# Hybrid RG-LRU, S5 and DeltaNet layer: the input scale moved into the S5 weights, the decay columns moved between RG-LRU tiles

## Chip, core and metric

The kernel runs on one core of a Trainium2 chip. The metric is the device time of one execution in microseconds (us), from the runs before: 1097.19 us median.

## What is computed

One layer of a recurrent decoder over 512 prompt and 64 sample positions (8 sequences of 8), 576 columns in all, with 1024 channels:

```python
h = rmsnorm(x, norm_pre_mix)
proj = h @ w_in      # rg_x, rg_gate, s5_u, qkv, z, a_in, b_in, three merge gates
y_rg = (rglru(conv(rg_x)) * gelu(rg_gate)) @ rg_w_out      # gated linear scan
y_s5 = glu(gelu(Re(C s) + D u)) @ s5_w_out                 # complex diagonal scan of u = s5_u
g    = -exp(a_log) * softplus(a_in + dt_bias)              # decay logits, 4 heads
beta = sigmoid(b_in)
y_gd = (rmsnorm(gated_delta(conv(qkv), beta, g)) * silu(z)) @ gdn_w_out
x = x + rmsnorm((g_rg*y_rg + g_s5*y_s5 + g_gd*y_gd) @ w_out, norm_post_mix)
x = x + rmsnorm(swiglu(rmsnorm(x)), norm_post_ffn)
```

The new recurrent states are outputs too. Everything is float32.

## The kernel before

All activations are held transposed: 128 channels on the partitions, 576 positions along the free axis, worked on in two halves of 288. A weight tile of 128 output channels is loaded as 128x512 pieces; ACT rounds a piece to its high part (`wh`, L181), DVE subtracts to get the low part (`wl`, L182), and each product is three matmuls, high by high, high by low and low by high (L199 to L201), into one PSUM tile per half (`mm3`). The input `h` is split in the same way (`hh`, `hl`, L236 and L237).

A tile scheduler lays the instructions out: each engine has one queue that it works through in order, and where several instructions could go next, the one written earlier in the source goes first. PSUM is given out by tags: "mm" (3 buffers, `mmp`) for the large products, "sm" (3 buffers) for the S5 tiles `gtp`, `xp`, `s5yp` and others, "sr" (2 buffers, `sr`).

The **start** loads x (`xa`), the S5 weights (`wr`, `uw`) and two tables (`par`, `con`) on SP's queue. `x_sums` squares x and adds the squares up, and multiplies x in place by the norm's scale `g_pre` (L356, ACT). `x_rows` turns the sums into a row of 1/rms values (`cps`, L365; Newton steps on DVE that end in `rs_o`, L118; spread over the partitions by `rows`, L262). `x_h` multiplies x by that row and splits it (L374). `x_u` computes the S5 input `u`, four tiles of 128 channels for each half, by plain float32 matmuls of the unsplit weights with `xa` (L381), and multiplies the result by the row while it leaves PSUM (L382). `issue_after(marks)` keeps the later `x_u` matmuls behind those of `x_rows`.

Then **S5**: constants of the state-space model on DVE (`s5ar`, L465, and after it exponentials, sines and powers), and for each of four tiles a front (`s5_front`: `bl`, L614 to L616 on DVE; `gtp`, L626, transposes it on PE; `ktp`, L632; `xp`, L648) and a chain (`s5_chain`: scans `zs`, products `zt`, outputs `s5yp`, L699 and L700). The tiles of **RG-LRU** (`rg(0)` to `rg(3)`: a projection, a convolution L420, gate products `gps` L748, a scan L769, a split L236 and L237) follow in the source, then five **merge gates** (`gate`), then the **decay block** (L833 to L905): the eight a and b columns `abps` (L849), their transposes `abc` (L854), exponential and softplus series on 128x20 tiles (L128 and L134 to L160), `gcl` (L871), running sums on PE (`gcps`, L873 to L878), `bgp` (L901), and a store `bgd` (L905) that later loads `eg` and `bet` (L969) read back. Then the merge of the RG-LRU branch (`mg`, L802) and the GDN branch, which begins with the projection and convolution of q and k (`pad`, L407 to L409), `sqp` (L931) and decay products `dt` (L973).

Of the kernel before, what the change touches and what calls it, by code (L numbers as in the profile page):

```python
# [8 lines left out]
F32 = mybir.dt.float32  # L9
# [56 lines left out]
def hybrid_step(ctx: ExitStack, tc: tile.TileContext, i, o, dbg=None):  # L66
# [242 lines left out]

    def acc_tile(name):  # L310
        return ap_.tile([128, KT, NT], F32, name=name, tag="acc")
# [8 lines left out]
    def load_u(m):  # L320
        us_.append(T("u"))
        uw.append([])
        raw = wp.tile([128, KT, 128], F32, name=nm("wr"), tag="wr", bufs=2) if m < 2 else None
        for a in range(0, KT, KC):
            if m < 2:
                r = raw[:, a:a + KC, :]
            else:
                r = sp5.tile([128, KC, 128], F32, name=nm("uw"), tag="PS"[m % 2], bufs=6 - m % 2)
            yield SY.dma_start(r, i["w_in"][IDX["u"] + m][:, a:a + KC, :])
            uw[m] += [r[:, k, :] for k in range(KC)]  # L330

    def load_c(t, src, a, b):
        yield SY.dma_start(t[:, a:b], i[src][:, a:b])

    xl, ul = [load_x(0), load_x(1)], [load_u(m) for m in range(4)]
    p0, p1 = load_c(par, "par", 0, NPAR - NHIST), load_c(par, "par", NPAR - NHIST, NPAR)
    c0, c1 = load_c(con, "con", 0, NCON - NLVL), load_c(con, "con", NCON - NLVL, NCON)
    for g_ in (p0, ul[0], xl[0], xl[0], ul[0], xl[0], xl[0], c0, ul[1], xl[1], xl[1], ul[1], xl[1], xl[1], ul[2], ul[2], ul[3], ul[3],
               p1, c1):
        next(g_, None)  # L340
# [6 lines left out]
    def x_sums(half):  # L347
        sl, sqs = hsl(half), sq_[half]
        for j in range(4):
            xv = xa[:, 2 * j:2 * j + 2, sl]  # L350
            if half and j % 2 == 0:
                S.activation(sqs[j], xv, AF.Square)
            else:
                V.tensor_tensor(sqs[j], xv, xv, op=OP.mult)
            for k in (2 * j, 2 * j + 1):
                S.activation(xa[:, k, sl], xa[:, k, sl], AF.Copy, scale=P("g_pre")[:, k:k + 1])  # L356
        V.tensor_tensor(sqs[0], sqs[0], sqs[1], op=OP.add)
        V.tensor_tensor(sqs[2], sqs[2], sqs[3], op=OP.add)
        V.tensor_tensor(sqs[0], sqs[0], sqs[2], op=OP.add)
# [11 lines left out]
    def x_h(half):  # L371
        for k in range(KT):
            t = R("h")[:, :NH]
            (G if half and k % 4 == 3 else V).tensor_tensor(t, xa[:, k, hsl(half)], rw_[half], op=OP.mult)  # L374
            split(t, h[k][0][:, hsl(half)], h[k][1][:, hsl(half)])

    def x_u(half, m, after=None):
        ps = mmp()
        with tc.issue_after(after) if after else nullcontext():
            for k in range(KT):  # L380
                PE.matmul(ps, uw[m][k], xa[:, k, hsl(half)], start=k == 0, stop=k == KT - 1)  # L381
        V.tensor_tensor(us_[m][:, 0:NT].rearrange("p (j c) -> p j c", j=8)[:, :, 36 * half:36 * half + 36],  # L382
                        ps.rearrange("p (c j) -> p j c", j=8), rw_[half].rearrange("p (c j) -> p j c", j=8), op=OP.mult)

    x_sums(0)
    x_sums(1)
    x_rows(0)
    x_h(0)
    x_u(0, 0)
    x_u(0, 1, marks[0])  # L390
    x_rows(1)
    x_u(0, 2, marks[1])
    x_u(0, 3, marks[2])
    x_h(1)
    for m in range(4):
        x_u(1, m, marks[3])
# [68 lines left out]
    V.tensor_tensor(ar[:, 0:NS], are, dts, op=OP.mult)  # L465
# [246 lines left out]
    V.tensor_scalar(nl_, P("rg_lam"), -1.0, None, op0=OP.mult)  # L712
# [95 lines left out]
    V.tensor_scalar(hb, P("glu_b"), 0.5, None, op0=OP.mult)  # L808
# [24 lines left out]
    rg_h = [rg(m) for m in range(3)]  # L833
    rg_h.append(rg(3))
    g1 = [gate(0, m) for m in range(5)]
# [15 lines left out]
    cps = pss.tile([128, 512], F32, name="abc", tag="sm")  # L851
# [18 lines left out]
    exp_cols(cp, nA, P("a_log"), 4)  # L870
    V.scalar_tensor_tensor(gcl, gcl, -1.0, nA[:, None, :].to_broadcast([128, 5, 4]), op0=OP.mult, op1=OP.mult)  # L871
    cps = pss.tile([128, 512], F32, name="gcps", tag="sm")
# [27 lines left out]
    bgp = pss.tile([128, 512], F32, name="bgp", tag="sm")  # L900
# [5 lines left out]

    DQ.dma_start(o["rg_h"], hout)
# [767 lines left out]
```

## Time and profile before

| | before |
|---|---|
| median of 3 runs | 1097.19 us (1095.03 to 1099.34) |
| profiled execution | 1097.05 us |
| its span | 1095.1 us |
| mean granted TensorE clock | 0.974 of full speed |
| PE busy | 1034.5 us, 94% |
| DVE busy | 795.3 us, 73% |
| ACT busy | 487.3 us, 44% |
| POOL busy | 231.0 us, 21% |

The span is the time between the first and last record of one execution; 1.95 us of the execution's time lie outside it. Matmul records overlap, since each lasts longer than the distance to the next one; the cost of a matmul in a full stream is the distance between starts. PE here is TensorE, DVE is VectorE, ACT is ScalarE, POOL is GpSimd, SP issues most of the loads. A plain float32 matmul leaves two records, the split ones leave one each.

### The profile page before, as it was taken

How to read it: one execution, taken by the hardware profiler on the slowest of the kernel's cores; microseconds unless marked ns; L12 is line 12 of the kernel's file. 1: busy time of each engine (PE TensorE's matmuls, PEld its weight loads, DVE VectorE, ACT ScalarE, POOL GpSimd, SP SyncE). 2: the span in 40 equal slices, each digit the busy share in tenths (PEclk: the TensorE clock that was granted, in tenths of full speed). 3: DMA queues.
4: the chain of work that ended last, by engine and by line, in shares of the span. 5: the costliest groups of instructions: out<-in, count | busy, mean ns of one | idle time of the engine just before them, and what ended most of it. 6: DMA issues, size and time to landing. Idle time of an engine off the chain costs nothing.

```text
span 1095.1 us, 20057 instructions
## 1 busy us (share of the span) xinstructions
PE 1034.5 (94%) x7658; PEld 988.9 (90%) x7658; DVE 795.3 (73%) x1853; ACT 487.3 (44%) x971; POOL 231.0 (21%) x301
## 2 busy tenths in 40 slices
PE   5999999967999999999999899899999999999994
PEld 4799989967989889998899899899999999999994
DVE  7899989876997678743636747875676776867756
ACT  4258943424443433222333444354653635536620
POOL 1024111104532234221001331210111201112114
PEclk8999999988999999999999999999999999999997
DMA  6333223422323133212112621124564646746602
GB/s 204 92 103 103 72 82 83 113 67 92 102 84 90 68 110 101 83 54 107 59 53 69 227 91 58 59 73 130 135 177 95 155 125 135 183 92 140 164 1 87
DMA packets 69521, 112.74 MB, mean 103 GB/s; under 512 B 27434, under 2 KB 35762, under 8 KB 69426
## 3 DMA queue, kind: packets, MB, share of 16 engines
q1 hardware_dynamic: 61650, 97.31, 27.7%
q0 software_dynamic: 7776, 14.16, 8.0%
q8 instruction: 60, 0.98, 0.4%
q14 instruction: 35, 0.29, 0.1%
HBM read 103.20 MB, written 8.24 MB: 102 GB/s over the span
## 4 chain that ended last, share of the span: by engine, by line
PE 78%; DVE 12%; DMA 4%; ACT 3%; issue 2%; POOL 0%; SPq 0%; DVEq 0%; ACTq 0%; POOLq 0%
PE mm L199 11%; PE mm L200 11%; PE mm L201 11%; PE mm L1439 10%; PE mm L1441 10%; PE mm L1440 10%; PE mm L381 2%; DVE wl L182 2%; PE up L1183 1%; PE s5yp L700 1%; DMA wr<-in_w_gate 1%; PE gps L748 1%; PE s5yp L699 1%; ACT wh L181 1%; PE rows L262 1%
## 5 line engine op out<-in xcount | busy, mean ns | idle before, releaser
L181 ACT ACTIVATE wh<-wr 128x512 fp32r<-128x512 f32 x250 | 154.7, 628 | 221.8 <-PE mm L200 119.4
L199 PE MATMUL mm<-hh,wh 128*128 128x288 f32 x768 | 232.8, 304 | 6.8 <-ACT pad L407 5.4
L182 DVE TENSOR_TENSOR wl<-wr,wh 128x512 fp32r<-128x512 f32 x250 | 182.2, 736 | 77.9 <-ACT wh L181 75.5
L200 PE MATMUL mm<-hl,wh 128*128 128x288 f32 x768 | 231.2, 301 | 0.0
L201 PE MATMUL mm<-hh,wl 128*128 128x288 f32 x768 | 230.1, 300 | 0.0
L199 PEld LDWEIGHTS mm<-hh,wh 128*128 128x128 f32 x768 | 145.9, 190 | 12.7 <-ACT pad L407 5.7
L201 PEld LDWEIGHTS mm<-hh,wl 128*128 128x128 f32 x768 | 145.9, 190 | 2.8 <-issue 2.2
L200 PEld LDWEIGHTS mm<-hl,wh 128*128 128x128 f32 x768 | 146.0, 190 | 2.5 <-issue 1.7
L1441 PE MATMUL mm<-fh,wl 128*128 128x288 f32 x352 | 103.7, 295 | 0.0
L1439 PE MATMUL mm<-fh,wh 128*128 128x288 f32 x320 | 94.6, 296 | 0.0
L1440 PE MATMUL mm<-fl,wh 128*128 128x288 f32 x320 | 94.4, 295 | 0.0
L1441 PE MATMUL mm<-hfh,wl 128*128 128x288 f32 x288 | 84.5, 296 | 0.7 <-DMA wl<-in_w_gate 0.7
L1440 PE MATMUL mm<-hfl,wh 128*128 128x288 f32 x288 | 84.9, 295 | 0.0
L1439 PE MATMUL mm<-hfh,wh 128*128 128x288 f32 x288 | 84.8, 295 | 0.0
L199 PE MATMUL mm<-brh,wh 128*128 128x288 f32 x224 | 67.4, 305 | 4.3 <-DVE mg L802 1.8
L200 PE MATMUL mm<-brl,wh 128*128 128x288 f32 x224 | 68.1, 305 | 0.9 <-DVE brl L237 0.6
L201 PE MATMUL mm<-brh,wl 128*128 128x288 f32 x224 | 66.9, 299 | 0.0
L1441 PEld LDWEIGHTS mm<-fh,wl 128*128 128x128 f32 x352 | 66.1, 188 | 0.0
L1440 PE MATMUL mm<-t,wh 128*128 128x288 f32 x216 | 64.0, 297 | 0.0
L1441 PE MATMUL mm<-t,wl 128*128 128x288 f32 x216 | 63.7, 295 | 0.0
L1439 PE MATMUL mm<-t,wh 128*128 128x288 f32 x216 | 63.6, 295 | 0.0
L1439 PEld LDWEIGHTS mm<-fh,wh 128*128 128x128 f32 x320 | 60.0, 188 | 0.1
(501 smaller groups left out, 2575.9 us busy)
## 6 DMA issues: line engine op xcount, KB each, us to landing
wr<-in_w_in SPq DMA_DIRECT2D x48, 512.0 KB, 3.5
wr<-in_w_gate SPq DMA_DIRECT2D x22, 512.0 KB, 3.9
wr<-in_w_up SPq DMA_DIRECT2D x22, 512.0 KB, 4.2
wr<-in_w_down SPq DMA_DIRECT2D x20, 512.0 KB, 4.9
wl<-in_w_gate POOLq DMA_DIRECT2D x27, 256.0 KB, 4.5
wl<-in_w_up POOLq DMA_DIRECT2D x27, 256.0 KB, 4.3
wr<-in_w_out SPq DMA_DIRECT2D x8, 512.0 KB, 3.5
xa<-in_x SPq DMA_DIRECT2D x8, 288.0 KB, 6.3
```

The costliest lines, as they stand in the source:

```text
L181: S.activation(hi, raw, AF.Copy)
L182: (eng or lo_eng()).tensor_tensor(lo, raw, hi.bitcast(F32), op=OP.subtract)
L199: PE.matmul(acc, hi[:, k, :], xh[:, sl], start=k0 + k == 0, stop=False)
L200: PE.matmul(acc, hi[:, k, :], xl[:, sl], start=False, stop=False)
L201: PE.matmul(acc, lo[:, k, :], xh[:, sl], start=False, stop=k0 + k == n - 1)
L262: m0 = PE.matmul(rows[:, 96 * b:96 * b + 96], rc[:96, b:b + 1].to_broadcast([96, 128]), ident[:96, :96], start=True, stop=True).ins
L381: PE.matmul(ps, uw[m][k], xa[:, k, hsl(half)], start=k == 0, stop=k == KT - 1)
L699: PE.matmul(ypv[:, b_, :], tm[:, g, :], x[:, g, :], start=True, stop=False)
L700: PE.matmul(ypv[:, b_, :], cl[g // 4][:, g % 4, 1:9, :].rearrange("p d h -> p (d h)"), st[:, g, :], start=False, stop=True)
L1439: PE.matmul(acc, hi[:, k0 + k, :], xh, start=new and k == 0, stop=False, skip_group_check=not new)
L1440: PE.matmul(acc, hi[:, k0 + k, :], xl, start=False, stop=False, skip_group_check=not new)
L1441: PE.matmul(acc, lo[:, k0 + k, :], xh, start=False, stop=k == len(x) - 1, skip_group_check=not new)
```

## The change

Three things are edited.

**The start.** The scale `g_pre` is no longer applied to x. It is multiplied into the S5 weights in place (`u_gain`, 32 activations of 128x128 in place of 16 of 128x288), and into `h` by a scalar_tensor_tensor that stays on DVE for all 16 pieces (before, two of them went to POOL). The matmuls of `x_u` and its evacuation `x_u_out` are taken apart, and two of the eight products get PSUM tiles of the tag "sr", so that five can be under way before a row of 1/rms values exists. `issue_after` is gone. The `par` table is loaded in three pieces, the first of them (32 columns, with `g_pre`) ahead of all else; S5 weights go ahead of the second half of x; a one-column activation at the very start (`first`) brings in ACT's table. ACT takes six of the eight squares (before two).

**The constants.** `s5ar`, `nlam`, `hb` and `nA` now read `pc`, a tile of zeros that takes the buffer of the second `rs_o`; they stand behind the second half's row in DVE's queue.

**The decay block** stands after `rg(1)` and ahead of `rg(2)`, `rg(3)` and the five gates in the source, and `abc`, `gcps` and `bgp` take PSUM tiles of the tag "sr".

```diff
@@ -307,6 +307,11 @@
+    first = cp.tile([128, 1], F32, name="first")
+    V.memset(first, 0.0)
+    S.activation(first, first, AF.Square)
@@ -326,17 +331,18 @@
-            yield SY.dma_start(r, i["w_in"][IDX["u"] + m][:, a:a + KC, :])
+            d_ = SY.dma_start(r, i["w_in"][IDX["u"] + m][:, a:a + KC, :])
             uw[m] += [r[:, k, :] for k in range(KC)]
+            yield d_
...
-    p0, p1 = load_c(par, "par", 0, NPAR - NHIST), load_c(par, "par", NPAR - NHIST, NPAR)
+    pg, p0, p1 = (load_c(par, "par", a, b) for a, b in ((0, 32), (32, NPAR - NHIST), (NPAR - NHIST, NPAR)))
...
-    for g_ in (p0, ul[0], xl[0], xl[0], ul[0], xl[0], xl[0], c0, ul[1], xl[1], xl[1], ul[1], xl[1], xl[1], ul[2], ul[2], ul[3], ul[3],
-               p1, c1):
+    for g_ in (pg, ul[0], xl[0], xl[0], ul[0], xl[0], xl[0], p0, c0, ul[1], ul[1], xl[1], xl[1], ul[2], ul[2], xl[1], xl[1],
+               ul[3], ul[3], p1, c1):
@@ -348,12 +354,10 @@
-            if half and j % 2 == 0:
+            if half or j % 2:
                 S.activation(sqs[j], xv, AF.Square)
             else:
                 V.tensor_tensor(sqs[j], xv, xv, op=OP.mult)
-            for k in (2 * j, 2 * j + 1):
-                S.activation(xa[:, k, sl], xa[:, k, sl], AF.Copy, scale=P("g_pre")[:, k:k + 1])
@@ -371,29 +375,44 @@
-            (G if half and k % 4 == 3 else V).tensor_tensor(t, xa[:, k, hsl(half)], rw_[half], op=OP.mult)
+            V.scalar_tensor_tensor(t, xa[:, k, hsl(half)], P("g_pre")[:, k:k + 1], rw_[half], op0=OP.mult, op1=OP.mult)
             split(t, h[k][0][:, hsl(half)], h[k][1][:, hsl(half)])
-    def x_u(half, m, after=None):
-        ps = mmp()
-        with tc.issue_after(after) if after else nullcontext():
-            for k in range(KT):
-                PE.matmul(ps, uw[m][k], xa[:, k, hsl(half)], start=k == 0, stop=k == KT - 1)
+
+    def u_gain(m):
+        for k in range(KT):
+            S.activation(uw[m][k], uw[m][k], AF.Copy, scale=P("g_pre")[:, k:k + 1])
+
+    def x_u(half, m):
+        ps = sr("u")[:, 0:NH] if (half, m) in ((0, 3), (1, 0)) else mmp()
+        for k in range(KT):
+            PE.matmul(ps, uw[m][k], xa[:, k, hsl(half)], start=k == 0, stop=k == KT - 1)
+        return half, m, ps
+
+    def x_u_out(half, m, ps):
         V.tensor_tensor(us_[m][:, 0:NT].rearrange("p (j c) -> p j c", j=8)[:, :, 36 * half:36 * half + 36],
                         ps.rearrange("p (c j) -> p j c", j=8), rw_[half].rearrange("p (c j) -> p j c", j=8), op=OP.mult)
+    u_gain(0)
+    pu = [x_u(0, 0)]
     x_sums(0)
+    u_gain(1)
+    pu.append(x_u(0, 1))
     x_sums(1)
+    u_gain(2)
+    pu.append(x_u(0, 2))
     x_rows(0)
+    u_gain(3)
+    pu.append(x_u(0, 3))
+    for p_ in pu:
+        x_u_out(*p_)
     x_h(0)
-    x_u(0, 0)
-    x_u(0, 1, marks[0])
     x_rows(1)
-    x_u(0, 2, marks[1])
-    x_u(0, 3, marks[2])
+    pu = [x_u(1, m) for m in range(3)]
+    for p_ in pu:
+        x_u_out(*p_)
     x_h(1)
-    for m in range(4):
-        x_u(1, m, marks[3])
+    x_u_out(*x_u(1, 3))
...
-    V.tensor_tensor(ar[:, 0:NS], are, dts, op=OP.mult)
+    V.scalar_tensor_tensor(ar[:, 0:NS], are, pc[:, 0:1], dts, op0=OP.add, op1=OP.mult)
...
-    V.tensor_scalar(nl_, P("rg_lam"), -1.0, None, op0=OP.mult)
+    V.tensor_scalar(nl_, P("rg_lam"), -1.0, pc[:, 0:1], op0=OP.mult, op1=OP.add)
...
-    V.tensor_scalar(hb, P("glu_b"), 0.5, None, op0=OP.mult)
+    V.tensor_scalar(hb, P("glu_b"), 0.5, pc[:, 0:1], op0=OP.mult, op1=OP.add)
@@ -830,9 +849,7 @@
-    rg_h = [rg(m) for m in range(3)]
-    rg_h.append(rg(3))
-    g1 = [gate(0, m) for m in range(5)]
+    rg_h = [rg(m) for m in range(2)]
...
-    cps = pss.tile([128, 512], F32, name="abc", tag="sm")
+    cps = sr("abc")
...
-    exp_cols(cp, nA, P("a_log"), 4)
+    V.tensor_scalar(nA, P("a_log"), pc[:, 0:1], None, op0=OP.add)
+    exp_cols(cp, nA, nA, 4)
...
-    cps = pss.tile([128, 512], F32, name="gcps", tag="sm")
+    cps = sr("gcps")
...
-    bgp = pss.tile([128, 512], F32, name="bgp", tag="sm")
+    bgp = sr("bgp")
...
+    rg_h += [rg(m) for m in range(2, 4)]
+    g1 = [gate(0, m) for m in range(5)]
```

The decay block, and with it the S5 fronts, move on PE too. Before, the first S5 front stands among the products of the first merge gate (`mm_2072`, `mm_2073`):

```order
L201 MATMUL mm_2072<-hh_137,wl_2069 128x288
L199 MATMUL mm_2073<-hh_131,wh_2068 128x288
L626 MATMUL gtp_697<-con,bl_686 128x128 x4
L632 MATMUL ktp_703<-cl_691,bb_675 32x128 x4
L748 MATMUL gps_1859<-xc_1846,rgw_1849 128x288
```
and the running sums of the decay stand at the end of the S5 outputs, ahead of the next q or k tile (`mm_3098`):

```order
L699 MATMUL s5yp_1333<-s5x_1108,tm_1117 128x72
L700 MATMUL s5yp_1333<-st_1299,cl_1161 128x72
L873 MATMUL gcps<-gcl,con 128x16
L874 MATMUL gcps<-gcl,con 64x4
L875 MATMUL gcps<-gcl,con 128x16
L876 MATMUL gcps<-gcl,con 64x4
L878 MATMUL gcps<-con,gcl 128x8 x4
L901 MATMUL bgp<-con,bg 40x128
L931 MATMUL sqp_3005<-sq_3003,con 32x288 x2
L199 MATMUL mm_3098<-hh_123,wh_3089 128x288
```
After, the first front stands behind the products of all five gates (`mm_2500` is the last of them), at the first products of the merge (`mm_2575`):

```order
L200 MATMUL mm_2500<-hl_142,wh_2495 128x288
L201 MATMUL mm_2500<-hh_141,wl_2496 128x288
L199 MATMUL mm_2575<-brh_2553,wh_2571 128x288
L199 MATMUL mm_2576<-brh_2553,wh_2571 128x288
L645 MATMUL gtp_717<-con,bl_706 128x128 x4
L199 MATMUL mm_2610<-brh_2553,wh_2606 128x288
```
the running sums stand between the first S5 tile's `xp` products and the gate products of `rg(2)`:

```order
L667 MATMUL xp_773<-s5x_681,gm_716 128x72 x2
L667 MATMUL xp_773<-s5x_681,gm_739 128x72 x2
L891 MATMUL gcps_1851<-gcl,con 128x16
L892 MATMUL gcps_1851<-gcl,con 64x4
L893 MATMUL gcps_1851<-gcl,con 128x16
L894 MATMUL gcps_1851<-gcl,con 64x4
L896 MATMUL gcps_1851<-con,gcl 128x8 x4
L919 MATMUL bgp_1879<-con,bg 40x128
L767 MATMUL gps_2027<-xc_2021,rgw_2024 128x288
```
and the place where they stood reads:

```order
L200 MATMUL mm_3118<-hl_142,wh_3114 128x288
L201 MATMUL mm_3118<-hh_141,wl_3115 128x288
L951 MATMUL sqp_3026<-sq_3024,con 32x288 x2
L199 MATMUL mm_3119<-hh_127,wh_3110 128x288
L200 MATMUL mm_3119<-hl_128,wh_3110 128x288
```
What moved: the decay's PE work stands some 450 instructions earlier, the S5 fronts some 240 later. Between the first front (instruction 690) and the first front of tile 3 (instruction 780) PE has 90 instructions, 36 of them large products; before, 466 instructions lay between those two (448 and 914), most of them large products. From `mm_3119` on (`mm_3098` before) the two programs have the same order.

On DVE the constants that read `pc` stand behind the second row (`rs_o`):

```order
L118 SCALAR_TENSOR_TENSOR rs_o_307<-rs_a_310,rs_y_309 96x3
L182 TENSOR_TENSOR wl_1381<-wr_1378,wh_1380 128x512
L182 TENSOR_TENSOR wl_1385<-wr_1378,wh_1384 128x512
L461 MEMSET s_z 128x3
L463 TENSOR_SCALAR par<-par,s_z 128x48
L182 TENSOR_TENSOR wl_1449<-wr_1446,wh_1448 128x512
L484 SCALAR_TENSOR_TENSOR s5ar_436<-par,s_z,s_dt 128x48
L731 TENSOR_SCALAR nlam<-par,s_z 128x4
L827 TENSOR_SCALAR hb<-par,s_z 128x4
L535 TENSOR_TENSOR s_ci<-par 128x48
L887 TENSOR_SCALAR nA<-par,s_z 128x4
```
Before, `s5ar` and `nlam` stood ahead of the first row:

```order
L712 TENSOR_SCALAR nlam<-par 128x4
L717 TENSOR_SCALAR rgc<-par 128x4
...
L128 SCALAR_TENSOR_TENSOR ex_r_621<-ex_r_621,ex_x_619 128x4
L465 TENSOR_TENSOR s5ar_416<-par,s_dt 128x48
L357 TENSOR_TENSOR sq_143<-sq_143,sq_144 128x576
```
What moved: the constants' whole chain, which stood around the Newton steps of both rows, starts after the second.

## Rows read from the trace of the kernel before

**Rows 1.** The page, busy time of each engine and its instructions.
```profile
PE 1034.5 (94%) x7658; PEld 988.9 (90%) x7658; DVE 795.3 (73%) x1853; ACT 487.3 (44%) x971; POOL 231.0 (21%) x301
```

**Rows 2.** Busy time by stretch: PE, PEld, DVE, ACT, POOL, clock, DMA.
```profile
0.00:52.60 52.60, 40.16 (x163) 31.68 (x164) 43.06 (x191) 19.75 (x41) 4.86 (x14) 0.90 0.46 148
52.60:120.00 67.40, 67.40 (x494) 65.69 (x493) 67.03 (x173) 48.50 (x94) 20.36 (x25) 1.00 0.32 97
189.80:233.50 43.70, 43.70 (x357) 42.58 (x355) 38.03 (x95) 16.63 (x34) 7.69 (x20) 1.00 0.35 92
233.50:247.80 14.30, 5.07 (x23) 3.66 (x22) 7.58 (x37) 4.57 (x13) 0.33 (x2) 0.59 0.29 71
247.80:263.60 15.80, 10.37 (x59) 10.14 (x58) 10.06 (x19) 6.78 (x15) 7.57 (x9) 0.72 0.31 111
```

**Rows 3.** Waits of PE in the first 320 us: total, times, longest.
```profile
PE gcps L873 <- DVE gcl L871: 7.1, 1, 7.1
PE mm L199 <- ACT pad L407: 5.4, 1, 5.4
```

**Rows 4.** Waits of DVE, 40 to 260 us, and the timeline of SP's queue.
```profile
DVE dt L973 <- DMA eg<-bgd: 6.6, 1, 6.6
...
239.60 1.86 SPq L707 DMA_DIRECT2D ys<-s5y  x4
...
247.41 0.42 SPq L969 DMA_DIRECT2D eg<-bgd  x1
```

**Rows 5.** Timeline of the start: start, length, instruction.
```profile
5.68 1.28 ACT L356 ACT_TABLE_LOAD   x1 [5.68 <-DMA xa<-in_x]
...
45.09 7.92 PE L381 MATMUL mm<-xa,uw 128*128 128x288 f32 x32
...
48.96 0.82 DVE L237 TENSOR_TENSOR hl<-h,hh 128x288 fp32r<-128x288 f32 x2
...
52.64 0.51 PE L199 MATMUL mm<-hh,wh 128*128 128x288 f32 x1
```

**Rows 6.** DVE's groups by form: the start, then 52.6 to 247.8 us.
```profile
L374 DVE TENSOR_TENSOR h<-xa,rows 128x288 f32<-128x288 f32 x14 | 5.9, 449 | 1.1 <-ACT rows L369 1.1
L354 DVE TENSOR_TENSOR sq<-xa 128x576 f32<-128x576 f32 x6 | 4.5, 754 | 1.6 <-DMA xa<-in_x 1.6
...
L182 DVE TENSOR_TENSOR wl<-wr,wh 128x512 fp32r<-128x512 f32 x41 | 27.9, 681 | 4.1 <-ACT wh L181 4.0
L802 DVE SCALAR_TENSOR_TENSOR mg<-gt,mm 128x288 f32<-128x288 f32 x14 | 6.2, 445 | 1.9 <-PE mm L201 1.9
L681 DVE TENSOR_TENSOR zt<-s_et,zs 128x256 f32<-128x256 f32 x8 | 3.3, 416 | 0.0
L128 DVE SCALAR_TENSOR_TENSOR sp_e<-sp_e,sp_a 128x20 f32<-128x20 f32 x7 | 1.3, 179 | 0.2
```

**Rows 7.** Timeline of PE in full streams.
```profile
53.12 0.29 PE L201 MATMUL mm<-hh,wl 128*128 128x288 f32 x1
53.25 0.29 PE L199 MATMUL mm<-hh,wh 128*128 128x288 f32 x1
...
218.04 0.39 PE L699 MATMUL s5yp<-s5x,tm 128*128 128x72 f32 x2
218.27 0.39 PE L700 MATMUL s5yp<-st,cl 128*128 128x72 f32 x2
```

**Rows 8.** Timeline around tile 3's first S5 front, DVE and PE.
```profile
189.15 0.68 DVE L616 TENSOR_TENSOR bl<-bl,tb 128x512 f32<-128x512 f32 x1
189.75 0.84 DVE L686 TENSOR_TENSOR st<-zt,zt 64x252 f32<-64x252 f32 x2
...
192.09 0.60 PE L626 MATMUL gtp<-con,bl 128*128 128x128 f32 x4
```

**Rows 9.** Timeline of PE behind the decay.
```profile
248.67 0.44 PE L199 MATMUL mm<-hh,wh 128*128 128x288 f32 x1
248.91 0.44 PE L200 MATMUL mm<-hl,wh 128*128 128x288 f32 x1
```

## Prediction

> **What bounds the kernel.** I read the page first: PE is busy for 94% of the span [rows 1], so a change gains only where PE stands still or runs slowly, and it loses wherever it opens a new hole. The view by stretches shows where that is, before 264 us [rows 2]. From 0 to 52.6 us PE is busy 40.16 us at a mean clock of 0.90. From 52.6 to 120 it is never idle, but DVE is full as well, 67.03 of 67.40 us; from 189.8 to 233.5 DVE still has 38.03 of 43.70. So in this half PE and DVE are nearly balanced, and a us of work more on DVE can become a us on PE's path. From 233.5 to 247.8 PE has 5.07 us of 14.3 at a clock of 0.59, and from 247.8 to 263.6 it has 10.37 of 15.8. The waits name both holes [rows 3]: 7.1 us for `gcl`, the end of the decay block's series on DVE, and 5.4 us for `pad`. The second has an earlier cause: DVE itself waited 6.6 us for the `eg` load [rows 4], which was issued at 247.41, as it reads what the decay block has stored. Both holes belong to the decay block, and the first 52.6 us to the start.
>
> **The start on PE.** The S5 input products take 7.92 us for 32 records [rows 5], and there are 64 products of two records: 31.7 us. Before, PE could begin only behind ACT's table load, released at 5.68 and 1.28 long [rows 5], and the scaling of x, and then met waits for the row. After, the table is loaded ahead of the data and five products need no row; with x landing at about the same 5.7 us, 31.7 us of products and some 3 us for `cps`, `rows` and a few short waits, the first large product comes at about 40.3 in place of 52.64 [rows 5]: 12.3 us earlier. That counts only if DVE keeps up.
>
> **The start on DVE.** Before, DVE is busy 43.06 of 52.6 us, 9.5 us idle [rows 2], and has the last `hl` at 49.8 [rows 5]. After, the second half of x lands behind more S5 weights, and its row stands behind more products, so I put the last `hl` at about 49 again. The chains of `s5ar` and `nlam` no longer fill DVE's waits before that: by the order of the two programs about 6.3 us of such work (exponentials and series at before's lengths) moves behind this point. The start then leaves DVE between 0 us behind (if everything comes 6.3 us earlier) and 6.3 us behind (if nothing does); I take **5.5**, as the second row's place on PE has hardly moved in time.
>
> **DVE up to the S5 fronts.** PE has 624 large products before its first S5 front and little else. A large product costs 0.13 us (53.12 to 53.25) [rows 7], so PE gets there by 40.3 + 90.5 = 131, and from there to tile 3's first front has only some 28 us of work. It could be there at 159. DVE is not: before, the `bl` that this front waits for ended at 189.8, and PE took it at 192.09 [rows 8]. A DVE instruction costs about 0.08 us less than its length, since the next one starts 0.60 us after a `bl` of 0.68 [rows 8]. Ahead of that `bl`, DVE now has
> - the decay block: 42 instructions on 20 columns of about 0.179 [rows 6], 7.5 us by length, +7.0 where some overlap (bounds: 4.2 if all overlapped by 0.08, 8.8 if each waited 0.03 for the last);
> - `h`: 16 of a 0.445 form (that of `mg`) for 14 of 0.449, +0.7; squares: 4 fewer of 0.754, -2.7;
> - 10 `mg` fewer, -3.65; 5 `wl` fewer, -3.0; 4 `zt` fewer, -1.3 (0.445, 0.681 and 0.416 long), since they are now ordered behind it [rows 6].
>
> That makes -2.9, with the 5.5 us of the start +2.6. So `bl` ends at 192.4, and PE has tile 3's first front at about **192.7**. In between PE stands still for about 32 us, which is where the 12.3 us of the start and the products taken out of this stretch go.
>
> **Charged at nothing.** The 32 gains of 128x128 on ACT, in place of 16 scalings of 128x288, lie beside products of 0.5 us each: ACT is busy for 19.75 of the first 52.6 us [rows 2], and only the first gain stands ahead of a product. If that cover goes, each product of the first round waits for its gain, at most some 5 us of the 12.3, which DVE hides here. The two PSUM tiles of the tag "sr" and the decay's 36 small matmuls, 4 us at the lower clock, move into a stretch where PE waits for DVE anyway. The table's third piece and the two POOL products of `h` are off every queue that ends a wait.
>
> **PE behind it.** From there to `mm_3119` PE has 348 large products at 0.132 (45.9 us), 46 `s5yp` of two records at 0.225 (218.04 to 218.27) [rows 7], 10.3 us, the remaining fronts, 3.5, and about 2.5 for `sqp`, short waits and the clock: 62.2 us, so `mm_3119` starts at 254.9. Before, its counterpart started at the end of the stretch to 247.8 [rows 2]. That is 7.1 us **later**, although the decay's hole of 14.3 us is gone.
>
> **What comes back.** Behind that point the order is the same. The decay is stored long before, so the 5.4 us for `pad` [rows 3] go; and the products that ran at 0.24 us apart (248.67 to 248.91) [rows 9] in place of 0.13, some 23 of them behind the two holes, give 2.5: together -7.9. What could be late next is `eg` again: on SP's queue its load now stands behind the `ys` stores of the last S5 tile, which took 1.86 us for four [rows 4]. I work it out to land just before DVE asks for it, so I charge nothing.
>
> **Sum.** +7.1 - 7.9 = -0.8 on the profiled execution's 1097.05 (1095.1 of it its span), which lies 0.14 below the median: 1096.2, rounded to **1096.0 us**. No difference that a measurement can tell: I take 0.5%, 5.5 us, as its limit.
>
> **A rule against the change.** In the stretch where PE had 5.07 us of work in 14.3 its granted clock was 0.59, and behind it products came at half rate [rows 2, 9]. So a PE that stands still for 32 us of 60 may do its small S5 products at 1.2 GHz. My sum charges 1.5 us for that. The Trainium skill ("TensorE: Matmul & The Clock Gate", Part 1: The HAM clock gate) says that the gate passes half of the pulses until the engine has been busy, and that there are two levels only; by that rule nearly all of this stretch would run at the lower level, and the result would be the slower rival below, 1103 us. The trace agrees in the one sparse stretch that it has.
>
> **Rivals.**
> *Slower: PE and DVE wait for each other through the S5 fronts.* With no large products between them, each front and each output is a round trip, at 1.2 GHz. The 28 us of PE work there would take 28 us more; where a quarter of it lies between a DVE instruction and the next one that needs it, DVE reaches `bl` 7 us later, at 199.4. The end is 1096.2 + 7 = 1103.2 us. For it: the clock of 0.59 [rows 2], and DVE idle for 13% from 189.8 to 233.5, where PE still had other work [rows 2]. Against it: DVE has the other RG-LRU tiles' and weights' work to do while it waits. It decides when DVE reaches that `bl` later than 197.4 (192.4 + 5.5 - 0.5).
> *Faster: DVE starts without the lag.* If the rows of both halves come as much earlier as PE does, the constants run in time that was idle before: -5.5 us, and less waiting for `wl` (4.1 us idle before them [rows 6]) up to -2: `bl` at about 185 to 187, the end at 1088 to 1091. For it: the 9.5 us that DVE idles in the start [rows 2]. Against it: h of the second half needs x, which lands later.
> *The decay moves, but `eg` still comes late.* If the last `ys` stores wait for their S5 tile, `eg` is issued as late as before against `pad`, and the 5.4 us stay [rows 3]: 1096.2 + 5.4 = 1101.6. That the block's placing does not do what it says is thus a case of its own.
>
> **Numbers.** My forecast 0.38, `eg` still late 0.07, slower rival 0.26, faster rival 0.29. The first two lie within 0.5% (1091.6 to 1102.7), so same 0.44; the faster rival and a start with no lag at all give faster 0.31; the slower one and a decay block at its upper bound 0.25. The range goes from 1085 (faster rival with the decay at 4.2 in place of 7.0) to 1106 (slower rival and 1.8 us for the block's upper bound): it leaves out under 2 in 10. The forecast's own range is 1091 to 1102.
>
> **What would show it.** Right: first large product at about 40; a stretch between 131 and 193 in which PE is busy for under half; tile 3's first `gtp` at about 193; `mm_3119` at about 255; no wait for `gcl` and none for `pad` of 5 us. Wrong: tile 3's first `gtp` before 188 or behind 198, a wait of DVE for `eg` of over 3 us, or a first large product behind 46.

## The result: 0.6% slower, and the profile after

The changed kernel takes 1104.1 us (median of 10 runs, 1099.69 to 1107.53) against 1097.2 us of the kernel before, run beside it (1094.81 to 1100.45): a ratio of 1.0057, 95% interval 1.0041 to 1.0074, 6.9 us slower. The forecast was 1096.0, no difference; the slower rival gave 1103.2, and the time lies inside the whole range of 1085 to 1106. The profiled execution after took 1106.39 us (span 1104.6), 2.3 above its median. The working below compares it with the profiled one before, 1097.05: 9.3 us to account for.

The page of the changed kernel, busy time and then PE and its clock in 40 slices of 27.6 us:

```profile
PE 1046.7 (95%) x7658; PEld 996.3 (90%) x7658; DVE 798.2 (72%) x1853; ACT 493.6 (45%) x992; POOL 228.3 (21%) x299
...
PE   8999986899989999999999899899999999999994
...
PEclk9999956899999999999999899999999999999997
```

The clock's line on the page of the kernel before:

```profile
PEclk8999999988999999999999999999999999999997
```

PE is busy 12.2 us *longer* than before with the same 7658 instructions [rows 1]. The clock's row says why: 5 and 6 in the slices from 138 to 193 us (the sixth and seventh digits), where the kernel before has 9 twice. A busier PE is here a slower one.

The same kernel by stretch (PE, PEld, DVE, ACT, POOL, clock, DMA):

```profile
0.00:52.60 52.60, 47.55 (x244) 39.90 (x245) 36.80 (x131) 26.24 (x65) 2.69 (x11) 1.00 0.53 169
52.60:120.00 67.40, 67.40 (x499) 65.18 (x498) 65.06 (x232) 45.39 (x88) 14.59 (x26) 1.00 0.28 84
131.00:193.00 62.00, 45.94 (x238) 35.81 (x236) 54.44 (x128) 34.94 (x72) 8.51 (x14) 0.63 0.19 49
196.60:206.00 9.40, 8.21 (x40) 7.97 (x41) 9.25 (x25) 1.23 (x2) 0.00 (x0) 0.64 0.22 61
206.00:261.60 55.60, 55.60 (x446) 54.26 (x444) 39.61 (x86) 22.93 (x46) 6.78 (x22) 1.00 0.42 116
```

The first row answers to the first of [rows 2]: PE has 7.4 us more done in the start, DVE 6.3 us *less* (36.80 for 43.06), and in the second row 2.0 less again. From 131 to 193 PE has the bare stretch, at 0.63 of its clock. The hole of 14.3 us before the running sums [rows 2] has no counterpart.

Its timeline, the places that the prediction named (start, length, instruction):

```profile
0.75 1.28 ACT L312 ACT_TABLE_LOAD   x1 [0.75 <-PEq L1685]
...
5.05 7.05 PE L389 MATMUL mm<-xa,wr 128*128 128x288 f32 x18 [5.05 <-DMA xa<-in_x]
...
41.84 0.51 PE L199 MATMUL mm<-hh,wh 128*128 128x288 f32 x1
...
50.73 0.44 DVE L237 TENSOR_TENSOR hl<-h,hh 128x288 fp32r<-128x288 f32 x1
...
134.12 0.66 PE L645 MATMUL gtp<-con,bl 128*128 128x128 f32 x4 [0.31 <-DVE bl L635]
...
195.75 0.68 DVE L635 TENSOR_TENSOR bl<-bl,tb 128x512 f32<-128x512 f32 x1
...
196.59 0.63 PE L645 MATMUL gtp<-con,bl 128*128 128x128 f32 x4 [1.78 <-DVE s5o L709]
...
261.62 0.40 PE L199 MATMUL mm<-hh,wh 128*128 128x288 f32 x1
```

They answer to [rows 5, 8]: the first large product 10.8 us earlier, the last `hl` 1.4 later, tile 3's first front at 196.59 where 192.09 stood, and `mm_3119` at 261.62, where its counterpart started at 247.8.

Waits of PE and of DVE, first 320 us (total, times, longest):

```profile
PE ktp L651 <- DVE cl L639: 7.8, 2, 5.6
...
PE gtp L645 <- DVE bl L635: 3.2, 4, 1.8
...
PE mm L199 <- ACT pad L426: 1.7, 1, 1.7
```
```profile
DVE wl L182 <- ACT wh L181: 7.5, 6, 2.4
...
DVE dt L993 <- DMA eg<-bgd: 1.8, 1, 1.8
```

The waits for `gcl` and the long one for `pad` [rows 3] are gone, DVE's wait for `eg` fell from 6.6 [rows 4] to 1.8. In their place PE waits for DVE's S5 fronts.

The decay is not stored earlier, though. PE, ACT and SP's queue, after:

```profile
148.91 0.40 PE L919 MATMUL bgp<-con,bg 128*40 128x128 f32 x1 [1.21 <-DVE bg L917]
...
241.33 0.27 ACT L921 ACTIVATE bgs<-bgp 40x128 f32<-40x128 f32 x1 [1.62 <-DVE s5o L707]
...
241.99 3.67 SPq L726 DMA_DIRECT2D ys<-s5y  x8
...
246.24 0.35 SPq L923 DMA_DIRECT2D bgd<-bgs  x1
...
255.18 0.42 SPq L989 DMA_DIRECT2D eg<-bgd  x1
```

PE has the block's last product at 148.91, but ACT copies it only at 241.33: in the source `bgs` takes one of the four SBUF buffers of the S5 products `zt` (tag "Z"), and the profile has the copy released by an S5 instruction, `s5o`. The store then stands behind eight `ys` stores: 246.24, hardly another time than that of the kernel before:

```profile
245.53 0.34 SPq L905 DMA_DIRECT2D bgd<-bgs  x1
```

The `eg` load is issued 7.8 us later than before; DVE's wait for it is short because DVE itself comes to `dt` later, at 260.94 for 252.49.

**A balance of PE.** I call the start of the first large product behind the first `sqp` (`mm_3098`, after `mm_3119`) the meeting point. Up to there PE has the same work in both. Summed over stretches of 1 us, busy time multiplied by the clock gives the work at full clock, and the rest of the busy time is the clock's loss:

| | meeting point | work at full clock | lost to the clock | idle |
|---|---|---|---|---|
| before | 247.8 | 215.1 | 8.3 | 24.4 |
| after | 261.6 | 215.8 | 21.7 | 24.1 |

Up to 45 us the change gains 11.5 us (16.5 of idle and clock before, 5.0 after). From 130 us on it loses 24.5: 40.7 (21.7 clock, 19.0 idle) against 16.2 (4.2 and 12.0), the decay's hole among the latter. From 206 us to the meeting point PE is busy without a break at the full clock (55.60 of 55.60 us above), so the whole of the loss lies between 130 and 206 us, in the fronts.

### The profile page after: what moved, and what is told of

Its sections match the earlier page's. It is cut to its first block, busy times and chain, and to the rows that moved or that the text cites. A ratio compares the mean times of both kernels' runs of the same rounds, so it can differ in the third digit from the quotient of the medians.

```text
span 1104.6 us, 20066 instructions
## 1 busy us (share of the span) xinstructions
PE 1046.7 (95%) x7658; PEld 996.3 (90%) x7658; DVE 798.2 (72%) x1853; ACT 493.6 (45%) x992; POOL 228.3 (21%) x299
## 4 chain that ended last, share of the span: by engine, by line
PE 59%; DVE 7%; DMA 3%; issue 1%; ACT 1%; DVEq 0%; POOL 0%; SPq 0%; ACTq 0%; POOLq 0%
PE mm L1461 10%; PE mm L1459 10%; PE mm L1460 10%; PE mm L199 8%; PE mm L200 7%; PE mm L201 7%; DVE wl L182 1%; DMA wl<-in_w_gate 1%; PE up L1203 1%; DMA ub<-bu 1%; DMA wr<-in_w_gate 1%; DVE x L1324 1%; DVE sqx L1308 1%; PE tps L1143 0%; PE zq L1185 0%
## 5 line engine op out<-in xcount | busy, mean ns | idle before, releaser
L1460 PEld LDWEIGHTS mm<-fl,wh 128*128 128x128 f32 x320 | 60.1, 188 | 0.0
```

The source lines that it names most:

```text
L1460: PE.matmul(acc, hi[:, k0 + k, :], xl, start=False, stop=False, skip_group_check=not new)
```

## The experiments

Each run was timed beside the kernel before. The table holds what the text needs: the ratio to the kernel before with its interval, and from the one profiled execution the meeting point, PE's loss to the clock and idle up to there, the end of the first `bl`, the end of the last S5 output (`s5y`), and DVE's wait for `eg`. Work at full clock is 214.6 to 217.2 in all but the one with added work (244.8). One execution can lie several us from its kernel's median (that of start_only took 1114.08, 6.3 below it), so its columns show where time is lost and do not add up to the medians.

| | median | ratio (95%) | meeting | clock, idle | first bl | last s5y | eg |
|---|---|---|---|---|---|---|---|
| before | 1097.2 | 1 | 247.8 | 8.3, 24.4 | 109.6 | 237.8 | 6.6 |
| after | 1104.1 | 1.0057 (1.0041 to 1.0074) | 261.6 | 21.7, 24.1 | 134.1 | 250.3 | 1.8 |
| start_only | 1120.4 | 1.0201 (1.0176 to 1.0226) | 262.5 | 16.4, 31.4 | 143.6 | 257.7 | 8.1 |
| decay_only | 1106.2 | 1.0082 (1.0067 to 1.0096) | 262.4 | 19.8, 27.1 | 106.3 | 234.2 | 2.0 |
| no_pc | 1107.9 | 1.0105 (1.0087 to 1.0123) | 251.9 | 11.5, 23.2 | 127.0 | 249.2 | 9.0 |
| end_sr | 1116.9 | 1.0173 (1.0153 to 1.0192) | 262.1 | 15.8, 31.6 | 143.6 | 259.5 | 8.9 |
| before_sr | 1094.2 | 0.9967 (0.9955 to 0.9980) | 241.8 | 5.6, 19.2 | 108.8 | 239.2 | 8.7 |
| no_pc_end | 1114.0 | 1.0143 (1.0125 to 1.0160) | 260.1 | 14.0, 30.3 | 138.0 | 257.5 | 8.6 |
| fill8 | 1120.9 | 1.0208 (1.0195 to 1.0221) | 275.4 | 10.3, 20.4 | 134.1 | 250.4 | 6.1 |
| before_pc | 1106.2 | 1.0072 (1.0056 to 1.0088) | 254.8 | 9.5, 28.7 | 129.2 | 250.0 | 8.2 |
| hold | 1117.6 | 1.0171 (1.0147 to 1.0194) | 271.9 | 14.7, 40.7 | 130.2 | 249.3 | 0.9 |
| eg_act | 1092.2 | 0.9950 (0.9932 to 0.9968) | 242.9 | 3.9, 21.7 | 109.4 | 238.6 | 2.1 |
| eg_pool | 1091.9 | 0.9945 (0.9924 to 0.9965) | 244.1 | 7.3, 20.6 | 109.4 | 241.5 | 1.2 |
| rg_behind | 1114.5 | 1.0167 (1.0141 to 1.0192) | 268.2 | 22.6, 30.5 | 131.5 | 240.0 | 1.9 |
| after_bc | 1112.5 | 1.0138 (1.0112 to 1.0163) | 258.3 | 16.4, 26.3 | 133.2 | 244.8 | 3.3 |
| egact_hi_front0 | 1099.2 | 1.0010 (0.9993 to 1.0028) | 246.2 | 4.6, 26.1 | 109.8 | 242.1 | 1.7 |

### The parts, one at a time

**start_only**: the change without its third part.

```diff
-    rg_h = [rg(m) for m in range(2)]
-    ...the decay block, with sr("abc"), sr("gcps"), sr("bgp")
+    ...
     g1 = [gate(0, m) for m in range(5)]
+    ...the decay block, on pss tiles of the tag "sm"
```

> The change without its third part: the decay block stands behind the gates again, on its old PSUM tiles. Theory A (bare fronts: the decay block and the held-back constants make DVE bring the S5 fronts late, PE has run ahead and does them without large products beside them, at the low clock): the first large product still comes at about 42 us, the last front of tile 3 stands among products of the merge again, the hole before the running sums of the decay (before: 233.5 to 247.8) is back, and the time is 1096 to 1101 us, between the two. Theory B (the decay block's DVE work alone is the loss, 7 us): at or below the kernel before, 1090 to 1097. Theory C (the start alone is the loss): as slow as the whole change, 1103 to 1106.

All three theories failed: it is far slower than the whole change. The last S5 outputs come after everything else is done, so PE's bare stretch has moved to 200 to 262 us, and the decay, with its `eg` load, is late again. PE meets only 0.9 us later than in the change; of the 7.7 us between the two profiled executions (1114.08 and 1106.39) the other 6.8 arise behind the meeting point, where PE waits 6.5 for `pad` (1.7 in the change). Stretch, then waits of PE and DVE, of this run:

```profile
200.00:262.00 62.00, 37.61 (x211) 33.84 (x209) 45.40 (x138) 16.86 (x41) 7.04 (x23) 0.56 0.23 51
```
```profile
PE s5yp L719 <- DVE st L705: 16.5, 3, 7.0
PE mm L199 <- ACT pad L426: 6.5, 1, 6.5
```
```profile
DVE dt L993 <- DMA eg<-bgd: 8.1, 1, 8.1
```

**decay_only**: the kernel before with the third part alone (the same lines moved, `nA` untouched).

> The kernel before with the third part alone: the decay block between RG-LRU tiles 1 and 2 on the other PSUM tiles, start and constants as before. Theory A: the last fronts are bare here too, but DVE brings them without the start's lag, the two decay holes are gone: 1093 if PE keeps its clock there, up to 1098 if it does not. Theory B: 1102 to 1106, the whole of the loss. Theory C: 1088 to 1093, a clear gain.

Slower too, where theory A gave at most 1098. Theory B's time (1102 to 1106) is nearly met, but not by more work ahead of the S5 chain, which comes earlier. The start's lag is absent (first `bl` at 106.3, the last `s5y` 3.6 us before the old time), yet the meeting point is 14.6 us later: the last four fronts have few products beside them, and PE loses 15.3 to the clock and 15.1 idle behind 130 us. So neither part is the loss alone, and the parts do not add up: the start with the held-back constants costs 23 us with the old decay, the decay 9 with the old start, and both together 7.

**no_pc**: the constants free again.

```diff
-    V.scalar_tensor_tensor(ar[:, 0:NS], are, pc[:, 0:1], dts, op0=OP.add, op1=OP.mult)
+    V.tensor_tensor(ar[:, 0:NS], are, dts, op=OP.mult)
...
-    V.tensor_scalar(nl_, P("rg_lam"), -1.0, pc[:, 0:1], op0=OP.mult, op1=OP.add)
+    V.tensor_scalar(nl_, P("rg_lam"), -1.0, None, op0=OP.mult)
...
```

> The change with its second part undone: s5ar, nlam, hb and nA no longer wait behind the second row. Theory A and the start's lag of the prediction (5.5 us on DVE): the constants fill DVE's waits in the start again, tile 3's first front comes at about 191 in place of 196.6, the time is 1098 to 1100. If the lag does not come from the constants: unchanged, 1102 to 1106, with the front at 195 to 197.

The first `bl` comes 7.1 us earlier and the meeting point 9.7, as the lag of the prediction had it. Tile 3's front did not move with it: 199.1 us, where 191 was expected and the change has 196.6. And `eg` is 9.0 us late, though its source was stored at 238.9: its load stood behind the last `ys` stores in SP's queue. The tail gives all of it back, and the kernel is 3.8 us slower than the change. **before_pc** puts the same four lines into the kernel before:

> The kernel before with the second part alone: s5ar, nlam, hb and nA wait behind the second row. Theory (the constants filled DVE's waits in the start): DVE is about 6 us behind at 50 us, the first S5 front comes some 6 to 12 us later than 113.4, fewer products are left to stand beside the last fronts, and the time is 1101 to 1110. If the held-back constants cost nothing: 1095 to 1099.

The first `bl` is 19.6 us later, the meeting point 7.0, the time 0.7% longer: within the range of the theory in the time, beyond it in the front. PE's first large product came at 44.83 in this run and at 44.10 in no_pc, for 52.64 before: the held-back constants without the new start, and the new start without them, each give PE most of its lead of 10.8 us, and with each the first `bl` is 17 to 20 us late.

**end_sr** and **no_pc_end**: the change with the decay block behind the gates, on the tiles of the tag "sr"; the second with free constants.

> The change with the decay block behind the gates in the source as before, but still on the other PSUM tiles. Theory A: the fronts stand among the merge's products again, the running sums are free of the S5 tiles and stand some 220 PE instructions earlier than on the old tiles, so both holes stay closed: the clock stays near 1.0 from 130 to 235 us, 1088 to 1096. Theory B (DVE's work ahead of the fronts): 7 us less ahead of them, 1096 to 1098. Theory C (the start): 1103 to 1106.

> The change with only its start (without the held-back constants) and the new PSUM tiles: the decay block behind the gates in the source, s5ar, nlam, hb and nA free. Against the run with one edit on the kernel before (the PSUM tiles alone) it shows the new start by itself. If the start is worth its 11 us on PE: 3 to 10 us faster than that run. If DVE sets the pace (theory of the prediction, DVE is no further at 50 us than before): no faster, and up to 10 us slower, as the fronts come later among products that PE has already done.

Both are much slower than the change, and theories A, B and C all missed end_sr (1116.9). no_pc_end against before_sr (below) shows the new start alone: 1114.0 to 1094.2, a loss of 20 us and not the 10 us allowed for, with the first `bl` 29 us later although PE's first large product is 7 us earlier. What DVE did until its first front ends shows what stands ahead of it. DVE's groups up to the first `bl`'s front, of the kernel before (to 109.6 us), then of the change (to 134.1):

```profile
L182 DVE TENSOR_TENSOR wl<-wr,wh 128x512 fp32r<-128x512 f32 x19 | 12.8, 680 | 0.0
L420 DVE SCALAR_TENSOR_TENSOR cv<-pad,par,cv 128x600 f32<-128x600 f32 x10 | 8.3, 830 | 0.0
```
```profile
L182 DVE TENSOR_TENSOR wl<-wr,wh 128x512 fp32r<-128x512 f32 x29 | 19.6, 680 | 4.0 <-ACT wh L181 4.0
L439 DVE SCALAR_TENSOR_TENSOR cv<-pad,par,cv 128x600 f32<-128x600 f32 x12 | 10.0, 829 | 0.5 <-ACT cv L437 0.5
```

Ten more weight splits (6.8 us) and two more RG-LRU convolution steps stand ahead of the first front. Summed over the records, DVE is busy 99.7 us up to the first `bl` before and 115.2 after, while up to *tile 3's* first front the change has 3.4 us less DVE work (172.9 to 169.5). So the work was reordered, and of the 24.4 us by which the first `bl` is late 17.8 are made up by tile 3's (196.4 for 189.8). That the splits are the cause is not shown: PE's stream of products asks for one about every 3 us in both kernels (19 by 109.6 us with the first large product at 52.6, 29 by 134.1 with it at 41.8), so a front that is late for another reason has more of them ahead of it too.

### Is it the clock, or DVE's S5 chain?

**fill8**: 128 more matmuls ahead of the fronts, which keep PE busy in the bare stretch.

```diff
+    def warm(ps, x):
+        for n in range(8):
+            PE.matmul(ps[:, 0:128], x, ident, start=True, stop=True)
...
             tps = pss.tile([128, 4, 128], F32, name=nm("gtp"), tag="sm")
+            warm(tps.rearrange("p a c -> p (a c)"), bb[:, 0].rearrange("p g h -> p (g h)"))
...
             kps = sm("ktp")
+            warm(kps, bl[:, 0].rearrange("p d h -> p (d h)"))
```

> The change with 128 more float32 matmuls of 128x128 (8 ahead of each gtp and each ktp group, on operands that DVE has just made, into the tile that is then overwritten): 28 us of extra PE work at full clock in the bare stretch, which adds nothing to the result. Theory clock (the slower rival of the prediction): PE stays at 2.4 GHz in most of the stretch, the waits of DVE for s5yp and of PE for the fronts shrink, tile 3's first front comes at 189 to 194 in place of 196.6, and the time is 1096 to 1103 in spite of the added work. Rival (the clock costs nothing there, DVE's own chain sets the pace): tile 3's front at 196 to 200, the time 1104 to 1110.

**hold**: the products of gates 2 to 4 held between the fronts; nothing added.

```diff
...
-        ps = w_in(IDX["gate"] + 8 * b + m)
+        ps = mm3(wload(i["w_in"][IDX["gate"] + 8 * b + m], KT), h, fmarks[2 * m - 3] if b == 0 and 2 <= m < 5 else None)
```

> The change with the products of merge gates 2, 3 and 4 (144 large ones, 19 us) held behind the S5 fronts' transposes, so that they stand between the fronts; nothing is added or left out. In the change PE's time up to the first q or k product behind the S5 outputs divides into 216 us of work at full clock, 21.7 us lost to the low clock and 24.1 us idle. Theory clock and cover: PE waits some 20 us for the first front at 130 to 134, but keeps the high clock in the stretch behind; the clock's loss falls from 21.7 to under 12, that product comes at 250 to 256 in place of 261.6, the time is 1094 to 1100. Rival (DVE's S5 chain sets the pace whatever PE does): the fronts and the outputs come when they came, the product at 259 to 264, the time 1102 to 1107.

The stretch from 131 to 193 us of fill8, then of hold:

```profile
131.00:193.00 62.00, 54.43 (x428) 49.73 (x426) 50.75 (x123) 34.19 (x71) 4.54 (x13) 0.92 0.18 46
```
```profile
131.00:193.00 62.00, 48.94 (x297) 42.60 (x297) 49.54 (x117) 33.18 (x69) 5.37 (x11) 0.74 0.20 48
```

and the last S5 output on DVE, of the change, of fill8 and of hold:

```profile
249.56 0.75 DVE L745 SCALAR_TENSOR_TENSOR s5y<-s5sq,s5y 128x576 f32<-128x576 f32 x1
```
```profile
249.63 0.76 DVE L751 SCALAR_TENSOR_TENSOR s5y<-s5sq,s5y 128x576 f32<-128x576 f32 x1 [0.36 <-ACT s5sq L750]
```
```profile
248.57 0.76 DVE L748 SCALAR_TENSOR_TENSOR s5y<-s5sq,s5y 128x576 f32<-128x576 f32 x1
```

The clock rose from 0.63 to 0.92 and 0.74, and the S5 chain ended within 1.0 us of where it had ended. Both readings of both runs missed the time (1120.9 and 1117.6), and hold's meeting point, 271.9, lies outside both as well. For the pace of the chain hold is the better witness: PE did 8 us more work (at full clock) in the stretch, and tile 3's first front came at 196.60, where the change has 196.59. So a clock of 0.74 in place of 0.63 did not hasten the fronts: there the rival's account is the right one. fill8 is no clean test: its added work stands in front of the real one, and tile 3's first front came at 206.5, outside both readings, so a gain by the clock and a loss by the queue could cancel in its chain's end. What the full clock throughout would give is not shown. Neither run gained: fill8 pays for its added work; in hold PE waited 16.0 us, idle, for the first `bl`, and had 43 more large products left at tile 3's first front (391 for 348).

**rg_behind** and **after_bc** ask what makes the chain late.

```diff
...
+            with tc.issue_after(after) if after and k == 1 else nullcontext():
-            V.scalar_tensor_tensor(y[:, :CW], pad[:, k:k + CW], w[k], y[:, :CW], op0=OP.mult, op1=OP.add)
+                V.scalar_tensor_tensor(y[:, :CW], pad[:, k:k + CW], w[k], y[:, :CW], op0=OP.mult, op1=OP.add)
```

> The change with the convolutions of the RG-LRU tiles held behind the S5 constants on DVE (by an order edge, nothing added). Theory (a), RG-LRU work among the constants delays the fronts: the last constant comes at 75 to 85 in place of 98.5, the first bl ends at 112 to 125 in place of 134.1, the S5 chain ends before 246 in place of 250.3. The whole then goes either way, as PE loses the early products' successors: 1098 to 1106. If the constants are held up by their own chain or by weight splits: first bl at 130 to 136, 1103 to 1110.

```diff
-        DQ.dma_start(bc4, i["s5_bc"][m])
+        nc.gpsimd.dma_start(bc4, i["s5_bc"][m])
```

> The change with the load of the S5 weights bc on POOL's queue in place of SP's, where it was issued at 121 us behind four weight loads that wait for buffers. Theory (b), the load's place holds the first front: first bl ends at 120 to 128 in place of 134.1 and the time falls by 4 to 10 us. If DVE's own order holds it (theory a): first bl at 132 to 136, the time within 3 us of the change's 1104.

With RG-LRU's convolutions held back, the last constant comes at 79.4 for 98.7, as theory (a) had it, but the first `bl` ends only 2.6 us earlier: the twelve convolution steps now stand between the constants and it, and 28 weight splits stand ahead of it (29 in the change). But the chain ends at 240.0, 10.3 us earlier, and *still* the kernel is slower: PE meets at 268.2, with 22.6 us lost to the clock and 30.5 idle, and from the second front to the last (137.6 to 201.8 us) PE has only 9 large products. The `bc` load on its other queue moves the first `bl` by 0.9 us: its place in SP's queue was not what held it. The meeting point is 3.3 us earlier there and the time yet 8 us longer: from there to the end its profiled execution took 852.9 us and the change's 844.8, so that loss, in these two executions, arises behind the meeting point. The 24.4 us of the first front are 15.5 us of work and 9.0 of idle time on DVE; which edit or wait weighs most in them is not settled.

### A faster version

**before_sr**: the kernel before, with `abc`, `gcps` and `bgp` on tiles of the tag "sr", and nothing else.

```diff
...
-    cps = pss.tile([128, 512], F32, name="gcps", tag="sm")
+    cps = sr("gcps")
...
```

> The kernel before with one edit: the decay's abc, gcps and bgp take PSUM tiles of the tag sr; the block stays behind the gates in the source, the start is the old one. The order is unchanged up to tile 2's second front; the running sums then stand some 140 PE instructions earlier. If the hole before the running sums comes from the decay's place behind the S5 tiles alone: the hole of 14.3 us closes to under 7, the first q or k tile behind it starts at 239 to 243 in place of 247.8, and the time is 1086 to 1093. If DVE's S5 work sets that point (it ended at 237.8): the tile starts at 243 or later and the time is 1093 to 1098.

The meeting point is 6.0 us earlier and the kernel 0.33% faster. The meeting point lies where the first reading had it, the time where the second had it: DVE's S5 work ends 1.4 us later than before, and the `eg` load is late. Queue of SP, then waits of DVE and PE, of this run:

```profile
230.60 0.34 SPq L905 DMA_DIRECT2D bgd<-bgs  x1
...
239.22 3.67 SPq L707 DMA_DIRECT2D ys<-s5y  x8
...
243.42 0.45 SPq L969 DMA_DIRECT2D eg<-bgd  x1
```
```profile
DVE dt L973 <- DMA eg<-bgd: 8.7, 1, 8.7
```
```profile
PE mm L199 <- ACT pad L407: 6.5, 1, 6.5
```

The source is stored at 230.6, but the load stands behind eight `ys` stores, which wait for the last S5 output. **eg_act** and **eg_pool** issue it elsewhere:

```diff
-            DQ.dma_start(t, bgd[5 * v:5 * v + 5].rearrange("n p -> (n p)")[None, 0:NT].to_broadcast([128, NT]))
+            nc.scalar.dma_start(t, bgd[5 * v:5 * v + 5].rearrange("n p -> (n p)")[None, 0:NT].to_broadcast([128, NT]))
```

> The kernel before with the decay's PSUM tiles of the tag sr (the run of that one edit: 1094.2), and the loads of eg and bet issued from ACT's queue in place of SP's, where they stood behind eight ys stores until 243.4 although their source was stored at 230.6. Theory: DVE's wait of 8.7 us for eg and PE's of 6.5 us for pad go, with some 2 us of half clock behind them: 1085 to 1089. If the loads' landing, not their place in the queue, is what is late: 1092 to 1096.

> As the run on ACT's queue, with the loads of eg and bet issued from POOL's queue: the same 1085 to 1089 where the place in SP's queue is the cause; later than that run where POOL's own order or its transfers hold them back.

Waits of DVE and of PE of eg_act:

```profile
DVE dt L973 <- DMA eg<-bgd: 2.1, 2, 1.0
```
```profile
PE mm L199 <- ACT pad L407: 2.7, 1, 2.7
```

The wait fell as expected, the time by 2 us where 5 to 9 were expected: 0.9950 and 0.9945 of the kernel before, the lowest here, but their intervals overlap each other's and that of before_sr. **egact_hi_front0** was to put the S5 constants and the first front ahead of the weight splits, by priority:

```diff
+    hp_ = tc.high_priority(offset=2 * HIPRI)
+    hp_.__enter__()
     ar = S5W("s5ar", NM)
...
+    hp_.__exit__(None, None, None)
     def s5_front(m):
...
-    fr = {0: s5_front(0)}
+    with tc.high_priority(offset=2 * HIPRI):
+        fr = {0: s5_front(0)}
```

> The faster version (old start, the decay's PSUM tiles of the tag sr, eg and bet on ACT's queue: 1092.2) with the S5 constants and the first front ahead of the weight splits in priority. If weight splits among the constants cost the chain time there: first bl 2 to 6 us before 109.4, 1086 to 1092. If not: 1090 to 1096.

It does not help: the first `bl` does not move (109.8), and the time is 7 us above eg_act. But it did not do what it was meant for: 19 weight splits stand ahead of the first `bl`, as many as before, and the constants even start later (`s5ar` at 17.0 for 13.3 in eg_act). Whether the splits hold the first front up stays untested.

## Why the prediction was wrong, point by point

The sum gave -0.8 us on the profiled execution, and it came out at +9.3. Three terms make up the 10.1: DVE reaches tile 3's front 3.9 us later than summed, PE needs 2.8 more behind it, and 3.4 less comes back.

- **The start on PE** was right: 41.84 for 40.3, 10.8 us earlier for 12.3. PE came to its first S5 front at 134.1 for 131; of the 90.5 us up to there the 624 products at 0.13 make 81, and the other 9 are not worked out in the prediction.
- **The start on DVE** was right in kind, low in size: 36.80 us done by 52.6 in place of 43.06, 6.3 behind for the 5.5 taken, and 8.2 behind at 120 us. The last `hl` ended at 51.2, not 49.
- **DVE's work ahead of tile 3's front**, -2.9, was right: -3.4.
- **Its idle time** is the first step that failed. The sum added the start's 5.5 us and kept all other idle time as it was. Summed over the records, DVE idled 16.9 us up to that `bl` before and 26.9 after, 10.0 more: 9.0 of them ahead of the first front (6.3 up to 52.6 us, 2.0 more up to 120; the waits for `wh` from ACT there are 4.0 us for none), 1.1 among the fronts. So `gtp` came at 196.6, 3.9 us behind the 192.7 of the sum. The step reads "So `bl` ends at 192.4"; it ended at 196.4.
- **PE behind it**, 62.2, measured 65.0 (196.6 to 261.6): the step's 2.5 us for clock, `sqp` and waits is the term that was too small, as 8.21 us at 0.64 alone lose 3.0, and 1.2 us of idle time came on top. So `mm_3119` is 13.8 us later, not 7.1.
- **What comes back**, 7.9, came to 4.5 at the end. Its premise, "The decay is stored long before", failed: the store came at 246.24, for 245.53 before. The trace gives 8.2 up to 264 us of the kernel before (the difference falls from 13.8 to 5.6). Then 2.0 are lost again, with a wait of 1.7 for `pad`, and the rest of the difference, to 9.3 at the end, arises in stages that the change does not touch; the median's 6.9 lies below it.
- **PE bare and at half rate** was foreseen as a stretch of 32 us idle and charged at 1.5 us of clock; it was 17 us at 0.63 of the clock (45.94 us busy, 37% of it lost) and 16.1 idle. By hold, both are for the most part one standstill: what the clock lost there, PE would have waited. The Trainium skill's rule ("TensorE: Matmul & The Clock Gate", Part 1: The HAM clock gate) foretold the lower level, and the trace agrees in the main: 0.63 in the stretch, between the half rate and the full one, and 1.00 again from 206 us.
- **The slower rival** gave the time, 1103.2 for 1104.1, but not by its mechanism. It had the round trips at 1.2 GHz delay DVE by 7 us, to be seen by a `bl` later than 197.4; it ended at 196.4. hold raised the clock, and tile 3's front came when it had come. What DVE lost, it lost nearly all ahead of the fronts (9.0 of the 10.0 us).
- **The faster rival** did not occur: its `bl` at 185 to 187 lies some 10 us too early. DVE idled 15.8 of the first 52.6 us, where that rival had it idle less than the 9.5 before.
- **The signs.** None of the three that were to show it wrong appeared (`gtp` at 196.6, `eg` 1.8 us, first product at 41.8), and two that were to show it right failed: `mm_3119` at 261.6 for 255, and PE busy for 74% of 131 to 193, not under half. The busy share hid the loss, as half-rate work counts as busy.
- **`eg` still late** did not happen in the change as a long wait (1.8 us), though the load came 7.8 us later than before; it did in six of the variants (8.1 to 9.0 us). In four of them (no_pc, before_sr, end_sr, no_pc_end) the source had been stored 11 to 15 us earlier, and the load stood behind `ys` stores; in start_only and before_pc the store itself came 2 us before the load.

What is shown: the change's early products are gained on PE (11.5 us) and given back (24.5 us) in a stretch in which PE has almost nothing but the S5 fronts, and DVE brings these late. decay_only shows that bare fronts do it even with a DVE that is not late. What stays open is which of DVE's waits and reorderings ahead of the first front weighs most; the held-back constants are worth 7 us of its end when they are taken out of the change (no_pc) and 19.6 when they are put into the kernel before (before_pc), so the 24.4 do not divide by edits.

## What to carry to other kernels

An engine that is made to run ahead takes its helpers with it: here ten more splits stood in the other engine's queue ahead of the first S5 front. Before moving work earlier, ask what is left to stand beside the slow chain later; here the same products were worth more there than at the start. And work moved earlier helps a later load only if the buffer of its result is free then (`bgs` came 92 us after the product that it copies), and if store and load don't stand behind stores that wait, in the same queue.

## What the runs showed that was not expected

Two edits that cost 23 us (the start with its constants) and 9 us (the decay block) alone cost 7 together; each moves the bare stretch to another place, which fits this but was not tested by itself. And a clock raised from 0.63 to 0.74 over 62 us was worth nothing to the fronts that PE was waiting for: there the lower rate was a sign of the standstill rather than its cause.
